# Two parts of an encoder's expert stage moved from VectorE to GpSimd: the gate-weighted one-hot rows and the low part of the activations

## The chip, the cores and the metric

The kernel runs on one core of a Trainium2 chip. The metric is device time in microseconds (us) of one execution, lower is better. Three executions of the kernel before took 2190.94, 2192.04 and 2187.36 us; their median is 2190.94 us.

## What is computed

The reference is an encoder of two layers on 256 tokens of width 1024. A layer is a token mixer (attention and pooling) and then an expert layer; the change touches the expert layer alone. Each token picks, for each of 8 heads, 16 of 16,384 experts, by two key lists of 128 (an expert's number is i*128 + j):

```python
s = jnp.einsum('bthpd,hpnd->bthpn', q, sub_keys)
vals, idx = lax.top_k(s, 16)
...
eidx = jnp.take_along_axis(cand_idx, pos, axis=-1)
g = jax.nn.softmax(top_s, axis=-1)
h = jnp.einsum('btd,bthkd->bthk', xblk, expert_u[eidx])
act = jax.nn.gelu(h) * g
y = jnp.einsum('bthk,bthkd->btd', act, expert_v[eidx])
```

## The kernel before

It doesn't gather experts. Per layer it computes the hidden value of all 16,384 experts for all tokens, multiplies it by a dense table of gates (zero where an expert was not chosen), and multiplies by all of expert_v. `peer` does it in stages; each layer runs them all.

- **First expert stage**, two halves `hf` of 64 products. A product (`transposed_product`, lines 98 to 102) loads 512 KB of expert_u, and 24 TensorE matmuls (line 96) make one column of hidden values for 128 experts. Two products share a PSUM tile, and ScalarE's Gelu (line 718) puts them into the half's SBUF tile `hb`.
- **Second expert stage**, 128 steps `i`: 512 KB of expert_v, and 12 matmuls of 512 columns (line 738) into four PSUM tiles.

All products run in split float32: an operand is a high part, which ScalarE makes, and a low part, which VectorE makes as the difference. For weights these are `wh` (line 74) and `wl` (line 75), two buffers each, from four load buffers `raw`, which SyncE's queue fills. In the second expert stage the activations are split too: every second step, line 731 (`xh`, ScalarE) and line 732 (`xl`, VectorE) split two columns of `hb` into 2 of 8 slots.

The gates are made by `gating(hb, i0)`, a generator that works through 32 groups of 8 tokens for each half. For a group, line 690 builds a one-hot row set over the 64 values of i (`pl[:, 1]`), and line 692, twice, multiplies it by the gate: first into `pl[:, 0]` by the gate's high part, then in place by its low part. Line 694 builds the one-hot rows over j (`ql`). 16 small matmuls on TensorE (line 697) turn both into gates in PSUM, and line 701 multiplies `hb` by them. `pl` and `ql` have two buffers each.

`work` paces that generator: it runs during the *other* work of TensorE, at 1.05 pieces a product, two pieces a group. So half 0's gates are made while the first expert stage works on half 1, and half 1's gates while the second stage takes steps 0 to 63. The small matmuls of a group stand in TensorE's queue between two big products, one product after the group's line 690 was emitted. `side` paces another generator in the same way, which computes modulation values of the next layer (in layer 0 only; a 512 KB load and the VectorE dot of line 143 each). The instructions of an engine run in the order in which a scheduler wrote them, and wait on semaphores.

Names for stretches below: **U2** is the first expert stage's second half (with gating), **V1** the second expert stage's steps 0 to 63 (with gating and line 732), **V2** its steps 64 to 127 (line 732 alone).

Of the kernel before, what the change touches and what calls it, by code (L numbers as in the profile page):

```python
# [9 lines left out]
F32 = mybir.dt.float32  # L10
# [5 lines left out]
ALU = mybir.AluOpType  # L16
# [33 lines left out]
def encoder_kernel(ctx, tc, x, c, ada_w, small, qkw, w_in1, w_in2, w_attn_o, mix_w, w_pool_o, w_out,  # L50
                   w_query, keys, expert_u, expert_v, band, rope, out, layers=NL):
    nc = tc.nc
    V, A, PE, G = nc.vector, nc.scalar, nc.tensor, nc.gpsimd
# [10 lines left out]
    def bank(tag):  # L64
        return psum.tile([P, 512], F32, name=tag, tag=tag, bufs=4 if tag == "y" else 2)
# [12 lines left out]
    def weights(src, shape):  # L78
        raw = rawtile()
        nc.sync.dma_start(raw, src)  # L80
        view = raw if len(shape) == 2 else raw.rearrange("p (a b) -> p a b", b=shape[2])
        if len(shape) == 4:
            view = raw.rearrange("p (a b c) -> p a b c", b=shape[2], c=shape[3])
        return split(view, shape)
# [136 lines left out]
    def xpair():  # L221
        return (xsp.tile([P, 8, S], F32R, name="xh", tag="xh"), xsp.tile([P, 8, S], F32R, name="xl", tag="xl"))
# [320 lines left out]
    def peer(l, arena, norm, side):  # L543
# [23 lines left out]
        xs = xpair()  # L567
# [108 lines left out]
        def gating(hb, i0):  # L676

            n = 64
            for t0 in range(0, S, TG):
                gp = bank("g").rearrange("p (t i) -> p t i", i=n)  # L680
                def row(a, m):
                    two = igj[:, a, t0:t0 + TG].rearrange("p (u v) -> p u v", v=2)
                    return two[:, :, None, :].to_broadcast([P, TG // 2, m, 2])

                def count(i, m):
                    return iota_t[:, None, i:i + m].to_broadcast([P, TG // 2, m, 2])

                ql = hot.tile([P, TG // 2, NK, 2], F16, name="ql", tag="ql")
                pl = hot.tile([P, 2, TG // 2, n, 2], F16, name="pl", tag="pl")
                V.tensor_tensor(pl[:, 1], count(i0, n), row(0, n), ALU.is_equal)  # L690
                for a in range(2):
                    V.tensor_tensor(pl[:, a], pl[:, 1], row(2 + a, n), ALU.mult)  # L692
                yield
                V.tensor_tensor(ql, count(0, NK), row(1, NK), ALU.is_equal)  # L694
                for t in range(TG):
                    for a in range(2):
                        PE.matmul(gp[:, t], ql[:, t // 2, :, t % 2], pl[:, a, t // 2, :, t % 2],  # L697
                                  start=a == 0, stop=a == 1)
                yield
                hv = hb[:, :, t0:t0 + TG]  # L700
                V.tensor_tensor(hv, gp.rearrange("p t i -> p i t"), hv, ALU.mult)  # L701
            yield

        hbs = []
        for hf in range(2):
            hb = half.tile([P, 64, S], F32, name="hb", tag="half")
            hbs.append(hb)
            for i2 in range(32):
                acc = bank("mm").rearrange("p (a t) -> p a t", t=S)
                for k in range(2):  # L710
                    transposed_product(expert_u[l, 64 * hf + 2 * i2 + k], xs, acc[:, k])
                    work(1.25 if hf == 0 else 1.05)
                    if hf:
                        side(0.3)
                if hf == 0 and i2 == 0:
                    key_scores(PH - 1)
                    work.gens.append(late)
                A.activation(hb[:, 2 * i2:2 * i2 + 2], acc, AF.Gelu)
            work.finish()
            work.gens.append(gating(hb, 64 * hf))  # L720

        xs = xpair()
        accs = [bank("y") for _ in range(4)]
        for i in range(128):
            hb = hbs[i // 64]
            if i == 64:
                work.finish()
            if i % 2 == 0:
                sl = slice(i % 8, i % 8 + 2)
                src = hb[:, i % 64:i % 64 + 2]  # L730
                A.activation(xs[0][:, sl], src, AF.Copy)  # L731
                V.tensor_tensor(xs[1][:, sl], src, xs[0][:, sl].bitcast(F32), ALU.subtract)  # L732
            wt = weights(expert_v[l, i], [P, D])
            todo = [(p, w, tt, d2) for p, w in ((0, 0), (1, 0), (0, 1)) for tt in range(NT) for d2 in range(2)]
            if i == 127:
                todo.sort(key=lambda a: a[2:])
            for p, w, tt, d2 in todo:
                PE.matmul(accs[2 * tt + d2], xs[p][:, i % 8, tt * P:tt * P + P],  # L738
                          wt[w][:, d2 * 512:d2 * 512 + 512], start=i + p + w == 0, stop=i == 127 and w == 1)
            work(1.05)  # L740
            side(0.15 if i < 64 else 0.62)
# [36 lines left out]
    for l in range(layers):  # L778
        parts = half.tile([P, 64 * S], F32R, name="parts", tag="half")
        arena = half.tile([P, 64 * S], F32, name="arena", tag="half")  # L780
        if l == 0:
            sig = arena[:, 0:D]
            A.activation(sig, c_b, AF.Sigmoid)
            V.tensor_tensor(c_b, c_b, sig, ALU.mult)
            ready(AF.Sqrt, sig[:, 0:1])
            keep_warm(WARM_START)
            first_ada = {n: ada_load(0, n) for n in (8, 9)}
            for k in range(2):
                nc.sync.dma_start(xT[:, 4 * k:4 * k + 4], x[:, 4 * k:4 * k + 4])
            first_ada.update({n: ada_load(0, n) for n in (0, 1)})  # L790
        norm = Norm(arena[:, 32 * 256:48 * 256])
        if l:
            residual(l - 1, accs, norm)
        norm = mixer(l, arena, parts, norm, Pace(ada_all(0, (2, 4, 3))) if l == 0 else Pace())
        side = [ada_all(0, (5,))] if l == 0 else []
        if l + 1 < layers:
            side.append(ada_all(l + 1, (1, 0, 2, 4, 3, 5)))
        accs = peer(l, arena, norm, Pace(*side))
# [82 lines left out]
```

## Time and profile before

| | us |
|---|---|
| median of 3 executions | 2190.94 (2187.36 to 2192.04) |
| the profiled execution | 2195.78 |
| its span, first to last instruction | 2194.0 |
| TensorE busy | 2154.1 (98%) |
| VectorE busy | 1610.6 (73%) |
| ScalarE busy | 1015.2 (46%) |
| GpSimd busy | 2.1 |
| mean granted TensorE clock | 0.989 of full speed |

The profile is one execution; its own time is 1.8 us over its span and 4.8 us over the median. Engines: PE is TensorE's matmuls, PEld its weight loads, DVE VectorE, ACT ScalarE, POOL GpSimd, SP SyncE. Busy times of PE are modelled and overlap, so a stretch in which PE is busy throughout says that no matmul waited, not that each ran at its best.

### The profile page before, as it was taken

Reading aid. Unit: us, or ns where it says so; the run is one execution under the profiler, and the core shown is the slowest. Engines: PE = TensorE matmul, PEld = TensorE weight load, DVE = VectorE, ACT = ScalarE, POOL = GpSimd, SP = SyncE. Lnnn points to the kernel's source line nnn. Section 1 sums busy time; section 2 is a strip of 40 time slices with the busy share of each in tenths; the row PEclk is TensorE's granted clock in tenths of the full one; section 3 lists DMA queues with packets and bytes.
Section 4 is the critical chain, followed back from the end, with each engine's and each line's share of the span. In section 5 each row is a group of like instructions: output and inputs, shape, how many; then the busy total and the mean of one; then the engine's idle time right before and its main releaser. Section 6 shows DMA issues by size and latency. Waiting matters only on the chain.

```text
span 2194.0 us, 38945 instructions
## 1 busy us (share of the span) xinstructions
PE 2154.1 (98%) x15738; PEld 1965.4 (90%) x15738; DVE 1610.6 (73%) x3086; ACT 1015.2 (46%) x1330; POOL 2.1 (0%) x9
## 2 busy tenths in 40 slices
PE   8999999999999999999999999999999999999998
PEld 6889999999999888877789999999999998888887
DVE  6878678846888899867666676796477778886554
ACT  3564445444444444444446644444444444444443
POOL 0000000000000000000000000000000000000000
PEclk8999999999999999999999999999999999999999
DMA  7767454555666666678745345545555555555563
GB/s 267 251 228 234 151 180 158 192 183 196 217 203 213 201 200 198 209 271 275 261 132 196 123 151 186 170 164 193 183 173 164 165 172 173 173 173 184 193 194 100
DMA packets 117093, 419.72 MB, mean 191 GB/s; under 512 B 13008, under 2 KB 14032, under 8 KB 116912
## 3 DMA queue, kind: packets, MB, share of 16 engines
q1 hardware_dynamic: 116784, 416.86, 57.9%
q8 instruction: 123, 2.02, 0.4%
q14 instruction: 58, 0.48, 0.1%
q0 software_dynamic: 128, 0.37, 0.0%
HBM read 416.13 MB, written 1.05 MB: 190 GB/s over the span
## 4 chain that ended last, share of the span: by engine, by line
PE 83%; DMA 7%; DVE 7%; issue 2%; ACT 2%; SPq 0%; DVEq 0%; ACTq 0%
PE mm L96 46%; PE y L738 27%; DMA raw<-in_ada_w_dram 5%; PE g L697 3%; DVE wl L75 3%; PE y L276 2%; PE g L598 1%; PE y L186 1%; PE y L96 1%; ACT wh L74 1%; DMA raw<-in_w_in_dram 1%; PE g L205 1%; DVE raw L143 1%; DMA raw<-in_expert_v_dram 0%; PE y L439 0%
## 5 line engine op out<-in xcount | busy, mean ns | idle before, releaser
L74 ACT ACTIVATE wh<-raw 128x1024 fp32r<-128x1024 f32 x680 | 719.9, 1059 | 1049.0 <-PE mm L96 549.6
L75 DVE TENSOR_TENSOR wl<-raw,wh 128x1024 fp32r<-128x1024 f32 x680 | 829.5, 1221 | 410.9 <-ACT wh L74 409.6
L96 PE MATMUL mm<-xh,wh 128*128 128x256 f32 x2816 | 700.5, 286 | 0.7 <-ACT wh L74 0.7
L96 PE MATMUL mm<-xl,wh 128*128 128x256 f32 x2816 | 691.6, 283 | 0.1
L96 PEld LDWEIGHTS mm<-xl,wh 128*128 128x128 f32 x2816 | 540.2, 192 | 2.4 <-DVE xl L231 2.1
L96 PEld LDWEIGHTS mm<-xh,wh 128*128 128x128 f32 x2816 | 539.7, 192 | 2.4 <-ACT wh L74 0.9
L96 PE MATMUL mm<-xh,wl 128*128 128x256 f32 x2816 | 398.3, 283 | 2.9 <-DVE wl L75 2.8
L96 PEld LDWEIGHTS mm<-xh,wl 128*128 128x128 f32 x2816 | 364.1, 192 | 4.9 <-DVE wl L75 4.6
L738 PE MATMUL y<-wl,xh 128*128 128x512 f32 x1024 | 277.5, 392 | 7.4 <-DVE wl L75 7.2
L738 PE MATMUL y<-wh,xh 128*128 128x512 f32 x1024 | 282.2, 396 | 0.5 <-ACT xh L731 0.5
L738 PE MATMUL y<-wh,xl 128*128 128x512 f32 x1024 | 274.8, 389 | 0.0
L738 PEld LDWEIGHTS y<-wl,xh 128*128 128x128 f32 x1024 | 191.2, 188 | 53.0 <-DVE wl L75 13.8
L738 PEld LDWEIGHTS y<-wh,xl 128*128 128x128 f32 x1024 | 192.4, 188 | 40.6
L738 PEld LDWEIGHTS y<-wh,xh 128*128 128x128 f32 x1024 | 187.9, 189 | 37.2 <-ACT xh L731 0.8
L143 DVE SCALAR_TENSOR_TENSOR raw<-raw,c_b 128x1024 f32<-128x1024 f32 x96 | 116.9, 1222 | 60.5 <-DMA raw<-in_ada_w_dram 60.3
L692 DVE TENSOR_TENSOR pl<-pl,igj 128x512 f16<-128x512 f16 x256 | 107.1, 419 | 2.5
L701 DVE TENSOR_TENSOR hb<-g,hb 128x512 f32<-128x512 f32 x128 | 87.4, 683 | 2.0 <-PE g L697 2.0
L732 DVE TENSOR_TENSOR xl<-hb,xh 128x512 fp32r<-128x512 f32 x128 | 87.1, 683 | 0.7 <-ACT xh L731 0.7
L694 DVE TENSOR_TENSOR ql<-iota_t,igj 128x1024 f16<-128x1024 f16 x128 | 87.4, 683 | 0.0
L697 PEld LDWEIGHTS <-ql 128*128 128x128 f16 x2048 | 68.5, 97 | 19.0 <-issue 16.2
L697 PE MATMUL g<-pl,ql 128*128 128x64 f16 x2048 | 83.7, 193 | 0.0
L731 ACT ACTIVATE xh<-hb 128x512 fp32r<-128x512 f32 x128 | 78.0, 615 | 4.9 <-DVE hb L701 3.8
(182 smaller groups left out, 1463.2 us busy)
## 6 DMA issues: line engine op xcount, KB each, us to landing
raw<-in_expert_u_dram SPq DMA_DIRECT2D x256, 512.0 KB, 3.6
raw<-in_expert_v_dram SPq DMA_DIRECT2D x256, 512.0 KB, 4.0
raw<-in_ada_w_dram SPq DMA_DIRECT2D x96, 512.0 KB, 4.4
raw<-in_w_in_dram SPq DMA_DIRECT2D x64, 512.0 KB, 4.5
raw<-in_w_query_dram SPq DMA_DIRECT2D x64, 512.0 KB, 3.9
raw<-in_w_attn_o_dram SPq DMA_DIRECT2D x16, 512.0 KB, 3.6
raw<-in_w_out_dram SPq DMA_DIRECT2D x16, 512.0 KB, 4.1
raw<-in_w_pool_o_dram SPq DMA_DIRECT2D x8, 512.0 KB, 3.9
```

Of the source, the lines that this page charges most:

```text
L74: A.activation(h, src, AF.Copy)
L75: V.tensor_tensor(lo, src, h.bitcast(F32), ALU.subtract)
L96: PE.matmul(acc, ws[k][w], xs[k][p], start=m == 0, stop=m == 3 * n - 1)
L143: V.scalar_tensor_tensor(raw, raw, 1.0, c_b, op0=ALU.mult, op1=ALU.mult, accum_out=mods[:, l, m:m + 1])
L276: PE.matmul(accs[tt], xs[p][:, 2 * dp + d, tt * P:tt * P + P], wt[w][:, d], start=dp + d + w + p == 0, stop=dp == 3 and d == 1 and (p if l ...
L692: V.tensor_tensor(pl[:, a], pl[:, 1], row(2 + a, n), ALU.mult)
L694: V.tensor_tensor(ql, count(0, NK), row(1, NK), ALU.is_equal)
L697: PE.matmul(gp[:, t], ql[:, t // 2, :, t % 2], pl[:, a, t // 2, :, t % 2], start=a == 0, stop=a == 1)
L701: V.tensor_tensor(hv, gp.rearrange("p t i -> p i t"), hv, ALU.mult)
L731: A.activation(xs[0][:, sl], src, AF.Copy)
L732: V.tensor_tensor(xs[1][:, sl], src, xs[0][:, sl].bitcast(F32), ALU.subtract)
L738: PE.matmul(accs[2 * tt + d2], xs[p][:, i % 8, tt * P:tt * P + P], wt[w][:, d2 * 512:d2 * 512 + 512], start=i + p + w == 0, stop=i == 127 ...
```

## The change

Two lines issue on GpSimd what they issued on VectorE. Nothing else is edited.

```diff
@@ gating(hb, i0)
                 V.tensor_tensor(pl[:, 1], count(i0, n), row(0, n), ALU.is_equal)
                 for a in range(2):
-                    V.tensor_tensor(pl[:, a], pl[:, 1], row(2 + a, n), ALU.mult)
+                    G.tensor_tensor(pl[:, a], pl[:, 1], row(2 + a, n), ALU.mult)
                 yield
@@ the second expert stage
                 A.activation(xs[0][:, sl], src, AF.Copy)
-                V.tensor_tensor(xs[1][:, sl], src, xs[0][:, sl].bitcast(F32), ALU.subtract)
+                G.tensor_tensor(xs[1][:, sl], src, xs[0][:, sl].bitcast(F32), ALU.subtract)
```

VectorE's queue in V1 of layer 0, before: `wl` is the weights' low part, `pl` and `ql` the one-hot rows, `hb` the gated hidden values, `xl` the activations' low part.

```order
L75 TENSOR_TENSOR wl<-raw,wh 128x1024
L701 TENSOR_TENSOR hb<-g,hb 128x64x8
L690 TENSOR_TENSOR pl<-iota_t,igj 128x512
L694 TENSOR_TENSOR ql<-iota_t,igj 128x1024
L692 TENSOR_TENSOR pl<-pl,igj 128x512
L732 TENSOR_TENSOR xl<-hb,xh 128x512
L75 TENSOR_TENSOR wl<-raw,wh 128x1024
L692 TENSOR_TENSOR pl<-pl,igj 128x512
```

The same queue and stage with the change:

```order
L690 TENSOR_TENSOR pl<-iota_t,igj 128x512
L694 TENSOR_TENSOR ql<-iota_t,igj 128x1024
L143 SCALAR_TENSOR_TENSOR raw,mods<-raw,c_b 128x1024
L75 TENSOR_TENSOR wl<-raw,wh 128x1024 x2
L701 TENSOR_TENSOR hb<-g,hb 128x64x8
```

The two rows of line 692 and the row of line 732 are gone from each turn; the others follow in the order they had.

GpSimd's queue at the start of V1 in layer 0, with the change; before, it holds nothing there. The names in brackets are the engines whose semaphores the instruction waits for.

```order
L732 TENSOR_TENSOR xl<-hb,xh 128x512 [waits PE_49,Activation_49]
L732 TENSOR_TENSOR xl<-hb,xh 128x512 [waits Activation_49] x2
L692 TENSOR_TENSOR pl<-pl,igj 128x512 [waits DVE_49,PE_49]
L732 TENSOR_TENSOR xl<-hb,xh 128x512 [waits Activation_49]
L692 TENSOR_TENSOR pl<-pl,igj 128x512 [waits Pool_49]
L732 TENSOR_TENSOR xl<-hb,xh 128x512 [waits Activation_49] x2
L692 TENSOR_TENSOR pl<-pl,igj 128x512 [waits DVE_49,PE_49]
L692 TENSOR_TENSOR pl<-pl,igj 128x512 [waits Pool_49]
L732 TENSOR_TENSOR xl<-hb,xh 128x512 [waits Activation_49]
```

Three `xl` are made ahead, and from then on a turn has the two `pl` and one `xl`. The first `pl` waits for VectorE's line 690, the second for the first. The queues of TensorE, ScalarE and SyncE are the same in both kernels.

## Rows read from the trace of the kernel before

**Rows 1.** The page's heading, its first part for PE, the chain that ended last.
```profile
span 2194.0 us, 38945 instructions
...
PE 2154.1 (98%) x15738; PEld 1965.4 (90%) x15738; DVE 1610.6 (73%) x3086; ACT 1015.2 (46%) x1330; POOL 2.1 (0%) x9
...
PE 83%; DMA 7%; DVE 7%; issue 2%; ACT 2%; SPq 0%; DVEq 0%; ACTq 0%
```
**Rows 2.** Windows: U2, V1, V2 of both layers: busy by engine, granted clock, DMA.
```profile
531.00:726.00 195.00, 195.00 (x1989) 193.62 (x1988) 165.55 (x262) 80.67 (x93) 0.00 (x0) 1.00 0.65 211
733.00:924.00 191.00, 191.00 (x1246) 155.16 (x1245) 174.80 (x280) 84.13 (x96) 0.00 (x0) 1.00 0.62 200
925.00:1100.00 175.00, 167.65 (x711) 132.88 (x710) 122.35 (x151) 77.11 (x88) 0.00 (x0) 0.99 0.79 267
1605.00:1799.00 194.00, 194.00 (x1980) 192.62 (x1979) 146.38 (x225) 79.49 (x91) 0.00 (x0) 1.00 0.51 166
1808.00:2000.00 192.00, 192.00 (x1250) 155.97 (x1250) 163.51 (x250) 85.06 (x98) 0.00 (x0) 1.00 0.53 174
2000.00:2150.00 150.00, 150.00 (x664) 124.20 (x663) 84.61 (x84) 72.49 (x83) 0.00 (x0) 1.00 0.60 194
```
**Rows 3.** Groups by line, whole span: busy us, mean ns, idle before.
```profile
L75 DVE TENSOR_TENSOR wl<-raw,wh 128x1024 fp32r<-128x1024 f32 x680 | 829.5, 1221 | 410.9 <-ACT wh L74 409.6
...
L692 DVE TENSOR_TENSOR pl<-pl,igj 128x512 f16<-128x512 f16 x256 | 107.1, 419 | 2.5
L694 DVE TENSOR_TENSOR ql<-iota_t,igj 128x1024 f16<-128x1024 f16 x128 | 87.4, 683 | 0.0
L701 DVE TENSOR_TENSOR hb<-g,hb 128x512 f32<-128x512 f32 x128 | 87.4, 683 | 2.0 <-PE g L697 2.0
L732 DVE TENSOR_TENSOR xl<-hb,xh 128x512 fp32r<-128x512 f32 x128 | 87.1, 683 | 0.7 <-ACT xh L731 0.7
...
L690 DVE TENSOR_TENSOR pl<-iota_t,igj 128x512 f16<-128x512 f16 x128 | 53.0, 414 | 0.0
```
**Rows 4.** Timeline of V1, layer 0: start us, duration us, instruction.
```profile
822.68 0.66 PE L697 MATMUL g<-pl,ql 128*128 128x64 f16 x16
...
825.03 0.41 DVE L690 TENSOR_TENSOR pl<-iota_t,igj 128x512 f16<-128x512 f16 x1
...
828.72 0.66 PE L697 MATMUL g<-pl,ql 128*128 128x64 f16 x16
```
**Rows 5.** Timeline of U2, layer 0.
```profile
563.93 0.65 PE L697 MATMUL g<-pl,ql 128*128 128x64 f16 x16
...
566.01 0.41 DVE L690 TENSOR_TENSOR pl<-iota_t,igj 128x512 f16<-128x512 f16 x1
...
570.26 0.65 PE L697 MATMUL g<-pl,ql 128*128 128x64 f16 x16
```
**Rows 6.** Groups by line on VectorE in U2 (two rows), then V1, of layer 0.
```profile
L690 DVE TENSOR_TENSOR pl<-iota_t,igj 128x512 f16<-128x512 f16 x34 | 14.1, 415 | 0.0
L143 DVE SCALAR_TENSOR_TENSOR raw<-raw,c_b 128x1024 f32<-128x1024 f32 x17 | 20.8, 1221 | 6.6 <-DMA raw<-in_ada_w_dram 6.4
L143 DVE SCALAR_TENSOR_TENSOR raw<-raw,c_b 128x1024 f32<-128x1024 f32 x10 | 12.2, 1221 | 1.3 <-DMA raw<-in_ada_w_dram 1.3
```
**Rows 7.** Groups by line on POOL: four of its nine instructions, all before 3.3 us.
```profile
masks.py:199 POOL TENSOR_SCALAR_AFFINE_SELECT ident<-ident 128x128 f32<-128x128 f32 x1 | 0.3, 300 | 0.0
L118 POOL IOTA iota<- 128x128 f32 x1 | 0.3, 257 | 0.0
masks.py:197 POOL MEMSET ident<- 128x128 f32 x1 | 0.2, 223 | 0.0
L872 POOL MEMSET const-float32-1.0<- 128x1 f32 x1 | 0.1, 98 | 0.0
```
**Rows 8.** Groups by line in V2 of layer 0: a PE row and a DVE row.
```profile
L738 PE MATMUL y<-wl,xh 128*128 128x512 f32 x238 | 66.6, 402 | 7.4 <-DVE wl L75 7.2
...
L143 DVE SCALAR_TENSOR_TENSOR raw<-raw,c_b 128x1024 f32<-128x1024 f32 x29 | 35.5, 1225 | 38.4 <-DMA raw<-in_ada_w_dram 38.4
```

## The prediction

> **What bounds the kernel now.** I read the page's first part and its chain first: TensorE is busy for 98% of the span, and 83% of the chain that ended last is its matmuls [rows 1]. A share over the whole span hides stages with other limits, so I then cut windows around the stages that the change touches [rows 2]. In U2 and V1 of both layers PE's busy time equals the window to the last digit (195.00 of 195.00, 191.00 of 191.00, 194.00 of 194.00, 192.00 of 192.00), at full granted clock; the same holds for V2 of layer 1. VectorE is nearly full there (174.80 of 191 in V1 of layer 0), but nobody on TensorE waits for it. Only V2 of layer 0 leaves TensorE time: 167.65 of 175. The reader is to see that VectorE at 91% is not the bound: taking work from it can give nothing where PE never waits.
>
> So two questions decide. Can the moved work be done on GpSimd in the time that the hidden place leaves? And does GpSimd leave VectorE alone while it works? For the first I read the timeline of one turn, the stretch between two sets of small gate matmuls. In V1 they start at 822.68 and 828.72, a turn of 6.04 us [rows 4]; in U2 at 563.93 and 570.26, a turn of 6.33 us [rows 5]. A U2 turn contains two products of 24 matmuls, a V1 turn two steps of 12. Line 690 ends at 825.44 (825.03 + 0.41) in V1, 3.28 us ahead of the matmuls that need both `pl`, and at 566.42 in U2, 3.84 us ahead. Into those gaps the two gate multiplications must now fit, one after the other, since the second overwrites what the first reads.
>
> **What is removed.** From VectorE go 256 of line 692 at 419 ns (107.1 us) and 128 of line 732 at 683 ns (87.1 us) [rows 3], 194 us of 1610.6. Worth on the path: nothing in U2, V1 and in V2 of layer 1, where TensorE never waited [rows 2]. In V2 of layer 0 at most the 7.4 us that its matmuls waited for `wl` [rows 8]; VectorE itself sat 38.4 us there behind loads of the modulation weights, which the change doesn't hasten. I take 0 for it.
>
> **What is added.** 384 instructions of 128 x 512 with two inputs on GpSimd, an engine that this trace shows only at its start [rows 7]. Its price has to be bounded from those rows. A memset of one column takes 98 ns, about 0.10 us of fixed cost; of 128 columns 223 ns, so a column written costs (223 - 98)/127 = 0.98 ns. The affine select, which reads one tile and writes one, takes 300 ns, 1.59 ns a column, so a column read costs 0.61 ns. Two reads and a write are 2.20 ns a column, and 512 columns take 0.10 + 1.13 = about 1.2 us. Lower end: as cheap as with one input, 0.10 + 512 x 1.59 ns = 0.9 us. Upper end: each input as dear as the whole select, 0.10 + 2 x 0.81 = 1.7 us. I take 1.2, which is composed of what the instruction does and lies nearest to the select's row. The Trainium skill (GPSIMD Engine Reference, section "Performance versus the Vector engine") has 4497 ns for such an operation on 2048 fp32 columns and advises VectorE for elementwise work; a quarter of it is an estimate of 1.12 us, by which the sum below would give 2283 us.
>
> **Where GpSimd and VectorE meet.** No row has the two engines at compute at once, so the cost of meeting is bounded from both sides. Below: nothing, they work side by side. Above: whatever reads two SBUF tiles on VectorE and whatever runs on GpSimd goes one after the other. I take the upper bound. VectorE's two-input operations run at the same 683 ns with both inputs in SBUF (line 732) as with one in PSUM (line 701) [rows 3], so they draw two SBUF streams at full rate, and a third and fourth stream from GpSimd must come from somewhere. That is a choice and no proof; the other bound stays as a rival. The Trainium skill (SBUF — State Buffer, section "Who interferes with whom") says it outright: GpSimd's only read port is VectorE's second one, and an instruction on either side holds it to its end. By that rule VectorE's line 701, with one input in PSUM, is free to run beside GpSimd. No run here shows either yet.
>
> **The sum, one after the other.** I follow a turn from the moment that the second `pl` is done and TensorE's gate matmuls start.
>
> - V1: the second `wl` 1.22; then `xl` on GpSimd 1.20, with line 701 (0.68) beside it; line 690 0.41; line 694 0.68; the first gate multiplication 1.20; the first `wl` of the next pair 1.22; the second multiplication 1.20. Together 7.13 us, against 6.04: TensorE waits 1.09 us at each set of gate matmuls. In layer 0 there are 10 dots of line 143 [rows 6] in 30 turns, 0.41 us more, so 1.50.
> - U2: the same without `xl`, and so with line 701 on the path: 1.22 + 0.68 + 0.41 + 0.68 + 1.20 + 1.22 + 1.20 = 6.61 against 6.33, 0.28 a turn. In layer 0, 17 dots [rows 6] in 34 turns add 0.61: 0.89.
> - Turns: of 128 groups [rows 3] 64 a layer, 34 in U2 [rows 6], so 30 in V1.
> - V2: `wl` twice and `xl` are 3.64 us; in layer 0 a dot a turn makes 4.9. A turn takes 150/28 = 5.4 us in layer 1 and 175/28 = 6.3 us in layer 0 (28 pairs of steps in each of the two windows [rows 2]). No cost: TensorE hides it.
>
> Sum: V1 30 x 1.50 + 30 x 1.09 = 78 us; U2 34 x 0.89 + 34 x 0.28 = 40 us; 118 us in all. The profiled execution's own time is 2195.78 us, so 2313.8; it stands 4.84 us above the median of the runs, so the forecast is **2309 us**. At 0.9 us for a GpSimd instruction the same sum gives 34 us (2225), at 1.7 us 276 us (2467).
>
> Who is queued behind: the gate matmuls stand in TensorE's queue ahead of the next step's 12 or the next product's 24 matmuls, so the whole stage stops with them; ScalarE's `wh` and the loads wait for the buffers that TensorE frees and shift along without cost of their own. A lower granted clock in the gaps would come on top; V2 of layer 0, with 4% of PE idle, still had 0.99 [rows 2], so I add nothing.
>
> **Rivals.** About 0.2% (4 us) is what a measurement of this kernel can tell from no change.
>
> *Side by side and hidden: no change, 2191 us.* A V1 turn has 3.6 us of GpSimd work in 6.04, and the two multiplications need 2.4 us plus two semaphore hops in gaps of 3.28 and 3.84 us. For it: full PE rows and VectorE relieved by 1.5 us a turn. Against: all three of price, chain and undisturbed VectorE must come out well, with 0.9 us to spare.
>
> *Side by side, but the chain is too long: slower by 5 to 30 us, about 2206.* At the upper price the two multiplications take 3.4 us and miss V1's gap of 3.28 by 0.15 us and the hops, say 0.25 us, in 60 turns: 15 us. It decides from 1.6 us an instruction. Against it: three rows on POOL point to less.
>
> *Faster: 2183 us.* In V2 of layer 0 VectorE, without 28 `xl` (19 us), is at its dots and `wl` sooner, load buffers come free sooner, and TensorE gets back most of the 7.4 us. It needs the engines to work side by side, and it decides if over half of that wait came from VectorE's queue. Against it: 38.4 us of VectorE idle on DMA [rows 8] say that the loads are late, not VectorE.
>
> That the change doesn't do what it says is excluded by the queues: 384 instructions have left VectorE and stand on GpSimd.
>
> **How the numbers follow.** One after the other has 0.58: the sum is above TensorE's turn in V1 for every price between the ends. Side by side and hidden has 0.24, side by side and too long 0.13, faster 0.05. Slower by over 0.2% is 0.58 + 0.13 = 0.71, the same 0.24, faster 0.05. The range begins at 2187, which takes in no change and leaves out most of the faster case (0.04), and ends at 2400, a GpSimd price of about 1.5 us (0.3 x (3 x 60 + 2 x 68) = 95 us above the forecast); I leave out some 0.12 above it. The forecast's own range is 2225 to 2400.
>
> **What would show it.** Right: PE's windows in V1 and U2 longer and with gaps, ended by POOL's `pl` ahead of line 697; V1 stretched more than U2, layer 0 more than layer 1, V2 unchanged; VectorE's `wl` starting later or lasting longer while POOL works; two `pl` that end 4 us or more after line 690. A wrong price shows as POOL starts less or more than 1.2 us apart where nothing else stands between. The whole is wrong if `wl` keeps its 1.22 us and its place while POOL's instructions run beside it.

## The result and the profile after

The changed kernel takes 2216.35 us (median of 4 executions, 2214.06 to 2219.09) against 2191.49 us (4 executions, 2187.36 to 2194.26): a ratio of 1.0116, 95% interval 1.0102 to 1.0131, or 25 us slower. The forecast said slower by 118 us. The direction was right, the size nearly five times too large; 2216 lies in the range, near its lower end. The profiled execution took 2219.09 us.

The page of the changed kernel: heading, busy times, and groups by line (busy us, mean ns | idle before, releaser).

```profile
span 2217.3 us, 39220 instructions
...
PE 2156.6 (97%) x15738; PEld 1960.6 (88%) x15738; DVE 1638.1 (74%) x2702; ACT 1018.0 (46%) x1330; POOL 669.6 (30%) x393
...
L75 DVE TENSOR_TENSOR wl<-raw,wh 128x1024 fp32r<-128x1024 f32 x680 | 971.0, 1436 | 400.0 <-ACT wh L74 397.0
...
L692 POOL TENSOR_TENSOR pl<-pl,igj 128x512 f16<-128x512 f16 x256 | 422.1, 1649 | 1258.6 <-DVE pl L690 1237.6
...
L732 POOL TENSOR_TENSOR xl<-hb,xh 128x512 fp32r<-128x512 f32 x128 | 247.7, 1937 | 248.2 <-ACT xh L731 248.2
L738 PE MATMUL y<-wl,xh 128*128 128x512 f32 x1024 | 279.5, 394 | 23.8 <-DVE wl L75 23.8
...
L697 PE MATMUL g<-pl,ql 128*128 128x64 f16 x2048 | 83.9, 193 | 0.9 <-POOL pl L692 0.9
```

Three things are to be seen against [rows 1, 3]. VectorE has lost 384 instructions and 194 us of work, yet is busy for 27.5 us *more*: line 75, which the change does not touch, went from a mean of 1221 to 1436 ns. GpSimd's 670 us for 384 instructions is no price either; a record of it contains waiting, as the timelines below show. And TensorE's new idle time is ended by `wl` from VectorE (23.8 us), not by GpSimd's `pl` (0.9 us): the gate products themselves are almost never late.

Where it lies is told by windows of the changed kernel. Columns: the window, its length, then busy us of PE, PEld, DVE, ACT, POOL, granted clock, DMA share, GB/s. The stretches are U2, V1 and V2 of layer 0 and V1 of layer 1.

```profile
525.00:725.00 200.00, 198.96 (x2017) 197.27 (x2016) 179.74 (x198) 81.68 (x95) 110.39 (x66) 1.00 0.64 207
725.00:940.00 215.00, 202.30 (x1314) 159.64 (x1313) 207.50 (x191) 89.82 (x103) 174.32 (x98) 1.00 0.57 183
940.00:1100.00 160.00, 147.24 (x626) 115.38 (x625) 110.41 (x115) 68.49 (x78) 42.66 (x26) 1.00 0.78 264
...
1850.00:1990.00 140.00, 140.00 (x940) 113.69 (x939) 139.84 (x118) 61.87 (x70) 128.31 (x72) 1.00 0.53 172
```

The same windows of the kernel before.

```profile
525.00:725.00 200.00, 200.00 (x2030) 198.62 (x2029) 170.59 (x275) 82.64 (x95) 0.00 (x0) 1.00 0.65 211
725.00:940.00 215.00, 214.74 (x1393) 175.50 (x1392) 191.38 (x302) 96.06 (x111) 0.00 (x0) 1.00 0.64 205
940.00:1100.00 160.00, 152.65 (x645) 120.48 (x644) 112.38 (x139) 70.82 (x81) 0.00 (x0) 0.99 0.79 267
```

PE's idle time is the second number less the third. In layer 0 it grew by 1.04 us in U2, 12.44 in V1 and 5.41 in V2, 18.9 in all. TensorE's idle time over the whole span grew by 20.8 us (2194.0 - 2154.1 = 39.9, 2217.3 - 2156.6 = 60.7), the span by 23.3. Layer 1's V1 loses nothing at all, although GpSimd works there for 128 of 140 us and VectorE is busy for 139.84 of 140. The granted clock is 0.99 or 1.00 in all these windows, so it has no part in this.

One pair of steps in that V1 of layer 1, VectorE's queue: start us, duration us, instruction.

```profile
1885.33 0.68 DVE L701 TENSOR_TENSOR hb<-g,hb 128x512 f32<-128x512 f32 x1
1885.92 0.92 DVE L690 TENSOR_TENSOR pl<-iota_t,igj 128x512 f16<-128x512 f16 x1
1886.76 0.68 DVE L694 TENSOR_TENSOR ql<-iota_t,igj 128x1024 f16<-128x1024 f16 x1
1887.37 4.04 DVE L75 TENSOR_TENSOR wl<-raw,wh 128x1024 fp32r<-128x1024 f32 x2
```

GpSimd's queue beside it.

```profile
1884.28 2.28 POOL L732 TENSOR_TENSOR xl<-hb,xh 128x512 fp32r<-128x512 f32 x1
1886.98 3.34 POOL L692 TENSOR_TENSOR pl<-pl,igj 128x512 f16<-128x512 f16 x2 [0.42 <-DVE pl L690]
1890.28 2.29 POOL L732 TENSOR_TENSOR xl<-hb,xh 128x512 fp32r<-128x512 f32 x1
```

`xl` is recorded from 1884.28 to 1886.56. The second `wl` of the turn before ended about 1885.4; from there `xl` needs 1.16 us, and it works while line 701, which has one input in PSUM, runs at its undisturbed 0.68 (all 128 records of line 701 lie between 675 and 692 ns). Line 690 then takes 0.92 instead of 0.41 [rows 3], because it has to let `xl` end. `ql` runs at 0.68 beside the first `pl`, which waits for it. The two `wl` take 4.04 together where 2 x 1.22 = 2.44 were due: each has one `pl` in front of it, and (4.04 - 2.44)/2 = 0.80 us, or 0.84 for a single one (2.06 less 1.22, in experiment 1 below), is what that `pl` holds VectorE up. From L701 to the next turn's L701 (1891.33) it is 6.00 us, and TensorE's turn is 6.04. So VectorE is full to within 0.04 us, and TensorE never notices.

The order can be the other way round: in V2 of layer 1 `wl` starts first, and `xl` waits.

```profile
2060.91 1.23 DVE L75 TENSOR_TENSOR wl<-raw,wh 128x1024 fp32r<-128x1024 f32 x1 [1.50 <-ACT wh L74]
...
2061.50 1.78 POOL L732 TENSOR_TENSOR xl<-hb,xh 128x512 fp32r<-128x512 f32 x1 [3.65 <-ACT xh L731]
```

`wl` keeps its 1.23 us and ends at 2062.14; `xl` ends at 2063.28, 1.14 us after that. Whoever starts first runs undisturbed, and the other waits until it is almost done: those 1.14 us are 0.15 less than the 1.29 us of the shortest `xl` of this trace. The Trainium skill (SBUF — State Buffer, section "Who interferes with whom") has this as a port that the two engines share and that an instruction holds to its end, with an input in PSUM left free; these rows agree in both directions but for such tenths of a us, and line 701's 0.68 beside `xl` agrees too.

In V1 of layer 0 a dot of line 143 comes on top. VectorE, one turn:

```profile
822.15 2.06 DVE L75 TENSOR_TENSOR wl<-raw,wh 128x1024 fp32r<-128x1024 f32 x1
824.54 1.65 DVE L143 SCALAR_TENSOR_TENSOR raw<-raw,c_b 128x1024 f32<-128x1024 f32 x1 [0.34 <-DMA raw<-in_ada_w_dram]
826.12 0.08 DVE L143 DVE_READ_ACCUMULATOR raw<-raw,c_b 128x1 f32 x1
826.12 2.30 DVE L75 TENSOR_TENSOR wl<-raw,wh 128x1024 fp32r<-128x1024 f32 x1
...
829.88 4.04 DVE L75 TENSOR_TENSOR wl<-raw,wh 128x1024 fp32r<-128x1024 f32 x2
```

TensorE there:

```profile
826.32 1.07 PE L738 MATMUL y<-wh,xl 128*128 128x512 f32 x4
828.48 1.19 PE L738 MATMUL y<-wl,xh 128*128 128x512 f32 x4 [1.09 <-DVE wl L75]
```

From first `wl` to first `wl` it is 7.73 us. `wl` itself waits behind the dot and behind the `xl` that slipped in after it (2.30 us), and TensorE stands still for 1.09 us. A turn that is full can catch up with almost nothing: V1 has eight dots, and seven of them are followed by such a wait of TensorE, of 0.50 to 1.65 us, which makes 7.6 of its 12.70 us of idle time. One more wait, of 0.93 us, has no dot just before it.

Another 2.1 us of it come at the end of V1, where the next layer's rotary tables (lines 298 and 301, small VectorE instructions that read two SBUF tiles) stand in VectorE's queue in front of `wl`. Two rows of VectorE, then two of TensorE:

```profile
922.25 0.29 DVE L298 TENSOR_TENSOR arena<-arena,qkw_b 128x128 f32<-128x128 f32 x1 [2.21 <-DMA arena<-in_rope_dram]
...
926.45 1.19 DVE L301 TENSOR_TENSOR arena<-arena,qkw_b 128x64 f32<-128x64 f32 x2
...
923.87 1.19 PE L738 MATMUL y<-wl,xh 128*128 128x512 f32 x4 [0.76 <-DVE wl L75]
...
928.83 1.20 PE L738 MATMUL y<-wl,xh 128*128 128x512 f32 x4 [1.35 <-DVE wl L75]
```

In the kernel before, the same tables cost TensorE nothing. The rest is 1.3 us at the start of the stage, where the kernel before loses 0.26, and 0.76 us behind the first dot of V2. Layer 1 has neither dots nor a next layer.

### The profile page after: what moved, and what is told of

Read it like the earlier page. It is cut to its first block, busy times and chain, and to the rows that moved or that the text cites. A ratio compares the mean times of both kernels' runs of the same rounds, so it can differ in the third digit from the quotient of the medians.

```text
span 2217.3 us, 39220 instructions
## 1 busy us (share of the span) xinstructions
PE 2156.6 (97%) x15738; PEld 1960.6 (88%) x15738; DVE 1638.1 (74%) x2702; ACT 1018.0 (46%) x1330; POOL 669.6 (30%) x393
## 4 chain that ended last, share of the span: by engine, by line
PE 48%; DMA 5%; DVE 3%; issue 1%; ACT 1%; POOL 0%; DVEq 0%; ACTq 0%
PE mm L96 24%; PE y L738 17%; DMA raw<-in_ada_w_dram 4%; PE y L276 2%; DVE wl L75 2%; PE g L697 1%; PE y L186 1%; DMA raw<-in_expert_v_dram 1%; PE g L598 1%; PE y L96 1%; PE g L205 1%; DVE raw L143 0%; ACT wh L74 0%; PE y L439 0%; PE y L415 0%
## 5 line engine op out<-in xcount | busy, mean ns | idle before, releaser
L75 DVE TENSOR_TENSOR wl<-raw,wh 128x1024 fp32r<-128x1024 f32 x680 | 971.0, 1436 | 400.0 <-ACT wh L74 397.0
L692 POOL TENSOR_TENSOR pl<-pl,igj 128x512 f16<-128x512 f16 x256 | 422.1, 1649 | 1258.6 <-DVE pl L690 1237.6
L732 POOL TENSOR_TENSOR xl<-hb,xh 128x512 fp32r<-128x512 f32 x128 | 247.7, 1937 | 248.2 <-ACT xh L731 248.2
L738 PE MATMUL y<-wl,xh 128*128 128x512 f32 x1024 | 279.5, 394 | 23.8 <-DVE wl L75 23.8
L143 DVE SCALAR_TENSOR_TENSOR raw<-raw,c_b 128x1024 f32<-128x1024 f32 x96 | 132.1, 1378 | 72.0 <-DMA raw<-in_ada_w_dram 71.7
L694 DVE TENSOR_TENSOR ql<-iota_t,igj 128x1024 f16<-128x1024 f16 x128 | 92.3, 721 | 0.0
L701 DVE TENSOR_TENSOR hb<-g,hb 128x512 f32<-128x512 f32 x128 | 87.0, 679 | 1.0 <-PE g L697 1.0
```

Of the source, the lines that this page charges most:

```text
L75: V.tensor_tensor(lo, src, h.bitcast(F32), ALU.subtract)
L143: V.scalar_tensor_tensor(raw, raw, 1.0, c_b, op0=ALU.mult, op1=ALU.mult, accum_out=mods[:, l, m:m + 1])
L692: G.tensor_tensor(pl[:, a], pl[:, 1], row(2 + a, n), ALU.mult)
L732: G.tensor_tensor(xs[1][:, sl], src, xs[0][:, sl].bitcast(F32), ALU.subtract)
```

## Experiments

The theory, **L**: instructions of VectorE with two SBUF inputs and GpSimd's go one after the other, and time is lost only where VectorE's work in a turn and what GpSimd holds it up exceed TensorE's turn, which is V1 of layer 0 with its dots, and V2 there. Rivals: **C**, GpSimd's two multiplications in a row make `pl` late; **O**, moving the instructions changed the queues' order and waits, and GpSimd's data traffic is harmless; **S**, both engines slow each other while they overlap. All ratios are against the kernel before, with 95% intervals.

### 1. The multiplications alone on GpSimd

```diff
-                G.tensor_tensor(xs[1][:, sl], src, xs[0][:, sl].bitcast(F32), ALU.subtract)
+                V.tensor_tensor(xs[1][:, sl], src, xs[0][:, sl].bitcast(F32), ALU.subtract)
```

> Theory L (lock): a VectorE operation with two SBUF inputs and a GpSimd operation that reads SBUF run one after the other, whichever starts first; a gate multiplication holds VectorE up 0.84 us, xl 1.16 us, and time is lost only where a turn's sum on VectorE passes TensorE's turn. With the gates alone on GpSimd and xl (0.6 us between starts) back on VectorE, a V1 turn is about 2.28 + 0.60 + 0.60 + 0.33 + 0.61 + 1.68 = 6.1 us, dots of layer 0 on top: V1 of layer 0 loses 8 to 14 us, layer 1 0 to 3, V2 nothing over the kernel before. 2200 to 2208 us, wl beside a gate multiplication about 2.06 us. Rival C (late gates, the chain of the prediction): the loss comes from TensorE waiting for the second gate multiplication; then nearly all of the change's 25 us stay (2210 to 2218).

2211.65 us (2205.39 to 2216.18, 6 executions), ratio 1.0094 (1.0072 to 1.0117): nearly 4 us above what L expected. VectorE's queue in V1 of layer 0:

```profile
806.98 0.68 DVE L694 TENSOR_TENSOR ql<-iota_t,igj 128x1024 f16<-128x1024 f16 x1
807.59 2.06 DVE L75 TENSOR_TENSOR wl<-raw,wh 128x1024 fp32r<-128x1024 f32 x1
809.56 1.52 DVE L732 TENSOR_TENSOR xl<-hb,xh 128x512 fp32r<-128x512 f32 x1
811.01 1.21 DVE L75 TENSOR_TENSOR wl<-raw,wh 128x1024 fp32r<-128x1024 f32 x1
...
813.68 2.06 DVE L75 TENSOR_TENSOR wl<-raw,wh 128x1024 fp32r<-128x1024 f32 x1
```

The mechanism is as L has it: a `pl` in front of `wl` (2.06) and one in front of `xl` (1.52 = 0.68 + 0.84), nothing in front of the second `wl` (1.21). But the turn is 6.09 us (807.59 to 813.68) and not below 6.04, so even turns without a dot lose a little, in layer 1 too (1.51 us of the 140 us window). TensorE is idle for 9.04 us in V1 of layer 0 and 7.42 in V2, where nothing changed from 7.35. C fits the time but not the rows: in V1 8.5 of the 9.04 us are ended by `wl`, and none by `pl`.

### 2. `xl` alone on GpSimd

```diff
-                    G.tensor_tensor(pl[:, a], pl[:, 1], row(2 + a, n), ALU.mult)
+                    V.tensor_tensor(pl[:, a], pl[:, 1], row(2 + a, n), ALU.mult)
```

> Theory L: with xl alone on GpSimd a V1 turn is 2.28 + 1.16 (line 701 beside it) + 0.33 + 0.61 + 0.80 = 5.2 us, 5.6 with layer 0's dots, under TensorE's 6.04: V1 loses nothing, U2 is as before, V2 of layer 0 loses the 5 to 10 us more that the changed kernel lost there, since wl and the dots wait for xl. 2196 to 2202 us. Rival S (both engines slow each other by sharing bandwidth all the time they overlap): wl is stretched in every stretch with xl, V2 of layer 1 included, by about the same factor.

2198.35 us (2194.15 to 2205.06, 12 executions), ratio 1.0027 (1.0014 to 1.0040), as L expected. V2 of layer 0:

```profile
940.00:1100.00 160.00, 149.23 (x629) 117.24 (x628) 111.71 (x116) 69.72 (x79) 47.33 (x26) 0.99 0.80 267
```

TensorE's idle time is 2.12 us in V1 and 10.77 in V2, 3.4 more than before. Of the 2.12, 1.66 lie behind 915 us, when the last gate matmuls (914.72) are done, so they belong to V2 too. The loss in V2 comes with `xl`, most of that in V1 with the multiplications. The profiled execution, of 2205.06 us, was the slowest of the twelve, so these windows say better where time goes than how much.

### 3. and 4. Both kernels without the dots in the second expert stage

`lite[0]` is true in the second expert stage; the lines that set it are left out here.

```diff
     def ada(l, m):
+        if lite[0]:
+            V.memset(mods[:, l, m:m + 1], 0.0)
+            return
         ada_dot(l, m, ada_load(l, m))
```

> The changed kernel with the modulation loads and dots of line 143 left out in the second expert stage (a memset of one column in their place; the modulation values made there are zero). Theory L: without the dots every turn fits; V1 and V2 of layer 0 look like those of layer 1, wl still about 2.06 us in V1. 2180 to 2190 us, and within 3 us of the kernel before with the same left out. Rival C: layer 0's V1 keeps its loss of some 10 us against that kernel.

> The kernel before with the same loads and dots left out: its 7.4 us in V2 of layer 0 go. 2180 to 2186 us. It is the base for the changed kernel without dots.

The changed kernel: 2182.94 us (median of 12 executions; 11 of them 2178.68 to 2187.55, one 3426.98), ratio 0.9963 (0.9950 to 0.9977). The kernel before: 2180.61 us (2171.60 to 2183.73, 9 executions), ratio 0.9944 (0.9925 to 0.9962). Without dots and their loads the change costs 2.3 us, which the two intervals don't tell from nothing, instead of 25. Windows of the changed kernel without dots, V1 and V2 of layer 0:

```profile
725.00:940.00 215.00, 212.07 (x1357) 171.82 (x1356) 196.13 (x175) 95.26 (x109) 178.41 (x98) 0.99 0.56 175
940.00:1100.00 160.00, 160.00 (x714) 132.67 (x713) 71.28 (x60) 76.97 (x86) 46.16 (x26) 1.00 0.60 185
```

GpSimd works just as long (178 and 46 us against 174 and 43), but TensorE is idle for 2.93 us in V1 where it was 12.70, and never in V2. C, by which V1 would keep its loss of some 10 us, falls. What is left in V1 comes from the rotary tables again: eleven of their instructions stand for 2.6 us in VectorE's queue ahead of a line 690, and the gate matmuls (line 702 of this kernel) wait for `pl`. Here C's mechanism does act. From 900 to 920 us:

```profile
L702 PE MATMUL g<-pl,ql 128*128 128x64 f16 x48 | 2.1, 193 | 2.2 <-POOL pl L697 2.2
```

### 5. The same GpSimd instructions without reading

```diff
-                    G.tensor_tensor(pl[:, a], pl[:, 1], row(2 + a, n), ALU.mult)
+                    G.memset(pl[:, a], 0.0)
-                G.tensor_tensor(xs[1][:, sl], src, xs[0][:, sl].bitcast(F32), ALU.subtract)
+                G.memset(xs[1][:, sl].bitcast(F32), 0.0)
```

> The changed kernel with a memset of the same tiles on GpSimd in place of the two multiplications and the subtraction (the gates and the low part are then zero): GpSimd writes and reads nothing; VectorE's queue stands as in the changed kernel. Theory L: no stretching, wl 1.22 us throughout, V1 of layer 0 full on TensorE, 2184 to 2193 us. Rival O (the new order of VectorE's queue costs, not GpSimd): the loss of some 10 us in V1 of layer 0 stays, 2205 us or more. Rival S (sharing by any activity): wl stretched beside the memsets too.

2191.26 us (2185.18 to 2194.60, 12 executions), ratio 0.9997 (0.9984 to 1.0011). Groups by line and form:

```profile
L75 DVE TENSOR_TENSOR wl<-raw,wh 128x1024 fp32r<-128x1024 f32 x680 | 830.6, 1222 | 556.4 <-ACT wh L74 553.4 <-PE g L355 1.9
...
L692 POOL MEMSET pl<- 128x512 f16 x256 | 134.1, 524 | 1533.1 <-DVE pl L690 1203.0 <-PE g L697 330.1
```

The 680 `wl` are back at a mean of 1222 ns, the longest at 1228, beside 384 GpSimd instructions of 524 to 527 ns each. O falls: it is the reading that holds VectorE up. It also says what the relief was worth: VectorE free of 194 us of work and undisturbed gains nothing that can be measured (V1 and U2 full as before, V2 idle for 5.51 us instead of 7.35).

### 6. One input instead of two

```diff
-                    G.tensor_tensor(pl[:, a], pl[:, 1], row(2 + a, n), ALU.mult)
+                    G.tensor_copy(pl[:, a], row(2 + a, n))
-                G.tensor_tensor(xs[1][:, sl], src, xs[0][:, sl].bitcast(F32), ALU.subtract)
+                G.tensor_copy(xs[1][:, sl], src)
```

> The changed kernel with copies of one tile in place of the three two-input operations on GpSimd (gates and low parts are then not what they should be). Theory L: a GpSimd operation that reads one tile holds VectorE's two-input operations for all of its own time as well: wl beside a copy is stretched by that copy's length and keeps 1.22 us where it starts first; 2190 to 2210 us by the copy's length. Rival S: half of the streams, so half of the stretching (wl about 1.6 us), also where wl starts first.

2194.03 us (2190.11 to 2198.28, 10 executions), ratio 1.0017 (1.0003 to 1.0030). The timeline in V1 of layer 1:

```profile
1880.27 1.23 DVE L75 TENSOR_TENSOR wl<-raw,wh 128x1024 fp32r<-128x1024 f32 x1 [1.16 <-ACT wh L74]
1880.67 1.29 POOL L692 COPY pl<-igj 128x512 f16<-128x512 f16 x1 [2.65 <-PE g L697]
...
1882.48 1.01 POOL L692 COPY pl<-igj 128x512 f16<-128x512 f16 x1 [0.52 <-DVE pl L690]
1883.44 0.61 POOL L732 CAST xl<-hb 128x512 fp32r<-128x512 f32 x1
1883.58 1.55 DVE L75 TENSOR_TENSOR wl<-raw,wh 128x1024 fp32r<-128x1024 f32 x1 [0.56 <-ACT wh L74]
```

A `wl` that starts first keeps 1.23 us; the copy that started 0.40 us later is recorded at 1.29, and the one behind line 694 at 1.01, where the shortest copy and the cast take 0.61: they waited. A `wl` that starts 0.14 us after a cast takes 1.55, so there it is `wl` that waited. S would have the first longer too. One input is enough for the meeting, but not for all of the instruction's time, as L had it: `wl` lost 0.33 us where 0.47 of the cast were left. With copies of 0.61 us V1 stays full (0.26 us idle, as before).

### 7. The loads without their dots

```diff
         if lite[0]:
+            ada_load(l, m)
             V.memset(mods[:, l, m:m + 1], 0.0)
```

> The changed kernel with the modulation loads kept in the second expert stage and only the dots of line 143 left out (the values are zero). Theory L: the dots' time on VectorE is what no longer fits in V1 of layer 0, so V1 is full on TensorE there; V2 of layer 0 keeps whatever the loads themselves cost. 2182 to 2192 us. Rival D (the loads' DMA time is the cause): as slow as the changed kernel, 2210 or more.

2190.91 us (2187.14 to 2194.48, 10 executions), ratio 1.0002 (0.9986 to 1.0018). TensorE is idle for 2.57 us in V1 and 5.07 us in V2. Against experiment 3 that puts V1's loss on the dots, not on their loads (2.93 without either, most of both from the rotary tables), while V2 is idle for 5 us with the loads alone: DMA carries 270 GB/s there instead of 185, and ScalarE's `wh`, which ends that idle time, waits for expert_v. In the changed kernel V2's idle time is ended by `wl` (11.9 us), so this doesn't say how its 12.76 us split between loads and dots.

### 8. to 10. The dots spread over earlier stages

If the dots make V2 idle, they belong where VectorE has room. Nothing is left out: some run in the query stage, more in the first expert stage, and few remain for V2. Once on the kernel before (8), once on the changed kernel (9), once on the changed kernel with line 692 on VectorE (10).

```diff
@@ queries
                 work(1)
+                side(0.3)
@@ first expert stage
-                    if hf:
-                        side(0.3)
+                    if hf or i2 >= 12:
+                        side(0.4 if hf else 0.3)
```

> The kernel before with layer 0's modulation loads and dots paced from the query stage on (0.3 a product there and in the late part of the first half, 0.4 in U2), so that V1 and V2 have nearly none; nothing is left out. By theory L's account of V2 of layer 0 its 7.4 us of waiting go: 2178 to 2188 us. If the loads collide with the weights' loads elsewhere instead: 2190 or more.

2181.08 us (2176.21 to 2185.37, 9 executions), ratio 0.9955 (0.9941 to 0.9969): 10 us faster than the kernel before, the best of all that keep the whole computation. V2 of layer 0 has 3 dots where it had 28, and TensorE is idle there for 0.40 us instead of 7.35:

```profile
940.00:1100.00 160.00, 159.60 (x713) 132.18 (x711) 90.24 (x93) 76.57 (x88) 0.00 (x0) 1.00 0.59 193
```

> The changed kernel with the loads and dots of layer 0 paced from the query stage on, as in v1_before_spread; nothing is left out. Theory L: V2 has nearly no dots and is full on TensorE; V1 still has some 9 dots in a turn that is full without them, each costing about 1.2 us; U2's turn has more dots than before, stretched by the gates. 2188 to 2200 us: most of the change's 25 us gone, slower than v1_before_spread (2181) by 7 to 19. Rival C: the loss against v1_before_spread stays 25 us or so.

2213.65 us (2210.73 to 2215.75, 4 executions), ratio 1.0107 (1.0093 to 1.0122): a miss. V2's idle time fell from 12.76 to 3.52 us, but U2's rose from 1.04 to 6.35, and V1's stayed at 11.63. U2 had 23 dots instead of 17. With GpSimd's holds on VectorE there was no room for 6 more, though it is recorded busy for only 177 of the 200 us. The same 23 dots in the kernel before (8) cost U2 0.59 us. The loss against experiment 8 is 32.6 us, more than the 7 to 19 of L and the 25 of C; the three stages' idle time accounts for 20 of it. It is not C's mechanism: in the whole execution the gate matmuls wait for `pl` for 2.1 us.

> The same with xl alone on GpSimd and the gate multiplications on VectorE. Theory L: a V1 turn of 5.2 to 5.6 us on VectorE and the lock under TensorE's 6.04, no dots in V2: no loss against v1_before_spread, 2179 to 2184 us. Nothing is won either, since TensorE is the bound.

2184.08 us (2174.85 to 2189.10, 12 executions), ratio 0.9964 (0.9949 to 0.9979), as expected. `xl` on GpSimd does no measurable harm once V2 is free of dots (0.82 us idle) and V1 has slack (0.94), and gives nothing over experiment 8 either.

### 11. and 12. No dots in V1

The rest of V1's loss should go if V1 has no dots, with nothing left out. The dots begin in the query stage and from pair 12 (product 24) of the first expert stage, as in 8, at a pace of 0.35; those lines are left out here.

```diff
-                        side(0.3)
+                        side(0.3 if hf else 0.35)
-            side(0.15 if i < 64 else 0.62)
+            side(0.0 if i < 64 else 0.3)
```

> The changed kernel with all work kept and layer 0's loads and dots paced so that V1 has none and U2 as many as in the kernel before (0.35 a product in the query stage and the late part of the first half, 0.3 in U2, 0 in V1, 0.3 in V2). Theory L: V1 is a full turn (6.0 of 6.04 us) and loses at most 3 us, U2 is as in the changed kernel (1 to 3 us), V2 has half its dots and loses 2 to 5 us: 2183 to 2193 us, within 3 to 9 us of the kernel before with the same pacing. If it is 2205 or more, something other than the dots' time beside GpSimd's is lost in V1.

2201.39 us (2197.10 to 2210.12, 7 executions), ratio 1.0046 (1.0029 to 1.0062): above the expectation, and 13.9 us above experiment 12, where 3 to 9 were expected. V1 did what it should: of the 175 us from 740 to 915 TensorE is idle for 0.90, where it was 7.73. But V2, with 16 dots where it had 31, is still idle for 7.22 us, and the stretch from 915 to 940 for 2.45, which are the rotary tables' again (2.2 us ended by `pl`). The profiled execution, of 2210.12 us, was the slowest of the seven.

> The kernel before with the same pacing; nothing left out. Every stage fits beside TensorE's turn: 2178 to 2186 us, like v1_before_spread (2181).

2187.53 us (2180.38 to 2190.96, 12 executions), ratio 0.9984 (0.9972 to 0.9997), 1.5 us above what was expected. With as many dots in V2, 16, TensorE is idle for 1.01 us there. So, as far as one execution of each shows, the dots in V2 cost more beside GpSimd's `xl`, and not in proportion to their number.

## Why the prediction was wrong in size

**What bounds it, and one after the other: right.** TensorE was full, VectorE's relief was worth nothing (experiment 5), and VectorE's operations with two SBUF inputs and GpSimd's do exclude each other, with line 701 free, as the forecast chose against its side-by-side rivals.

**The step that failed is the sum of the turn, first of all its price for an instruction of GpSimd.** The forecast put 1.2 us for each into VectorE's turn. Alone they take about that (shortest records: 1.10 us for `pl`, 1.29 for `xl`), but VectorE is held up for less: 0.80 to 0.84 us by a `pl`, 1.16 by an `xl`. That takes 0.76 us off V1's turn of 7.13 and leaves 6.37. The other 0.36 is an error that the trace of before could have shown: I added durations, while on VectorE each record runs some 0.08 us into the next one. In the kernel before, next to the L690 of [rows 4], L701 ends at 825.11, and L690 starts at 825.03:

```profile
824.43 0.68 DVE L701 TENSOR_TENSOR hb<-g,hb 128x512 f32<-128x512 f32 x1
```

Five such joints make 0.4, and the turn is the 6.00 us measured, just under TensorE's 6.04. So the loss in V1 of layer 1 is 0, not 30 x 1.09. In U2 6.61 shrinks to about 5.5 by the same reckoning, and even 17 dots in 34 turns fit: 1.04 us lost, not 30 in layer 0 and 10 in layer 1. What is left of the sum is V1 in layer 0, where dots of 1.22 us [rows 6] go onto TensorE: 10 of them would make 12 us. V1's idle time grew by 12.4, and that agreement is luck: the waits behind its eight dots make 7.6 of it, one more wait 0.9, the next layer's rotary tables, which the sum didn't have, 2.1, and the stage's two ends the rest. The sum was only 0.28 to 1.09 us longer than TensorE's turn, so errors of 0.36 us in each `pl` and 0.4 in the joints decided all of it; the low end of the price, 0.9 us, gave 34 us and was the better answer, though partly by luck: it put 10 us into U2 and none into V2.

**The gap from line 690 to the gate matmuls was misread.** I took 3.28 us [rows 4], as if `pl` were used by the next set of gate matmuls. Counting from 500 us to 828.60 in the kernel before, the first row is line 690, the second the gate matmuls on TensorE:

```profile
500.00:828.60 328.60, 20.71 (x50) 1.00 0.64 205
...
500.00:828.60 328.60, 31.34 (x768) 1.00 0.64 205
```

50 row sets were made, but 768/16 = 48 sets of matmuls done, so the set at 828.72 is the 49th and the `pl` made at 825.03 belongs to the 50th: the gap is a turn longer, 3.28 + 6.04 = 9.3 us. That is why TensorE waits for `pl` only 0.9 us in all, and why the sign of being right that I named, gaps ended by POOL's `pl` ahead of line 697, did not show. The wait moved to `wl`, in whose queue the holds add up. It also removes the ground of the rival with a chain too long.

**V2 of layer 0, costed at nothing: wrong by 5.4 us.** I took it that TensorE would hide 4.9 us of work in a turn of 6.3. The turn is 5.9: the window's 711 matmuls [rows 2] are 29.6 pairs of steps of 24, not 28. That alone still hides 4.9. But VectorE waits there 42.5 us for loads (34.0 before, from 940 to 1100 us), and what is late behind such a wait, as I read it, leaves no room for a hold; this is argued, not shown. That `xl` brings most of this loss is shown by experiment 2 (V2 worse, the gating in V1 not), that it needs the dots and their loads by 3 and 10. How the wait splits between dots standing in front of `wl` and load buffers freed later was not settled; experiment 12 against 11 only shows that it is not proportional to the dots.

**The faster rival** named the same place and asked that the engines work side by side; they don't. Even where they do, beside the memsets of experiment 5, V2 gets back only 1.84 of its 7.35 us. Nearly all of it could be had, but by moving the dots (experiment 8).

## What to carry to other kernels

Work moved from VectorE to GpSimd stays a load on VectorE if it reads SBUF, as far as VectorE's own instructions there read two SBUF tiles: add what it holds VectorE up (here 0.8 us of 1.1, and 1.16 of 1.29) to VectorE's turn, and compare that turn with the bounding engine's, stage by stage, before looking at busy shares. Add starts to starts, not durations, when turns come within a few per cent of each other, and count producers and consumers from the start of the stage before calling the distance between two rows a slack. If a stage is idle because of paced side work, moving that to a stage with room can be worth more than speeding up its neighbours (here 10 us against nothing that could be measured).

## What the hardware showed that I had not expected

- Records of both engines contain the wait for each other: `wl` reads 2.06 us and `xl` up to 2.34 for 1.22 and 1.29 us of work. A busy VectorE (207.50 of 215 us in V1) is then no measure of its work.
- A two-input instruction of GpSimd holds VectorE up for about 0.3 us less (`pl`) or 0.1 us less (`xl`) than it takes alone.
- A second input costs GpSimd 0.49 us on 512 columns (1.10 for `pl` against 0.61 for the copy of experiment 6, the shortest records of each), 0.96 ns a column if a multiplication and a copy differ in nothing else, where the forecast had drawn 0.61 ns from the affine select of [rows 7]. The Trainium skill (GPSIMD Engine Reference, section "Performance versus the Vector engine") led to an estimate of 1.12 us for two fp32 inputs; the shortest `xl` takes 1.29.
